# A hybrid attention, pooling and RWKV block on one core: moving the residual gate's matvec to the end of the mixers in half-width pieces, alternating two heads' transposes, and lengthening two planned delays

## The chip, the cores and the metric

The kernel runs on one core of a Trainium2 chip. The metric is the device time of one execution in microseconds. Of the kernel before there are three runs: 1617.52, 1618.55 and 1624.68 us, median 1618.55. The profile is of one more execution, which took 1624.09 us; its trace has a span of 1622.2 us.

## The reference, cut to what matters

One layer on 256 latent tokens with 256 context tokens in front, width 2048, all in float32.

```python
shift_l, scale_l, gate_l = adaln_modulation(c, w_mod, b_mod)   # silu(c) @ w_mod + b_mod, split in three
h = concat(rms_norm(x_ctx) * (1 + scale_c) + shift_c, rms_norm(x_lat) * (1 + scale_l) + shift_l)
parts = split(h @ w_in)                    # q, k, v, gates, pool input, rwkv r, k, v, merge logits ...
y_na = neighbourhood_attention(...)        # 16 heads of 64
y_pool = multiscale_pool(...)
y_rw = rwkv7(...)                          # 16 heads of 64, both directions, seeded by the context
merged = sum(sigmoid(merge_logits[b]) * ((y_b * silu(gate_b)) @ w_branch[b]) for b in range(3))
return rms_norm(x_lat + gate_l * (merged @ w_out), final_g)
```

The change is about three things in it: `gate_l`, a product of one row of 2048 values with a 2048 x 2048 third of `w_mod` that is only needed at the very end; the RWKV part; and the attention.

## The kernel before, in words

The work stands in four stages. **First**, until about 149 us, the modulation's shift and scale are computed piece by piece and the normalised input `hh`, `hl` (a high and a low part of each float32 value) is made for all 16 row blocks. **The mixers**, from 149 to about 1390 us, hold all projections by `w_in` and the three branches. **The merge** multiplies by `w_branch` until about 1528 us, and **the output** by `w_out` until the end.

A projection tile of the mixers (`column_tile`, line 721) is cut in four units. A unit loads 256 KB of weights into a buffer `raw` (line 565), ACT casts it to `whi` (L568), DVE makes the rest `wlo` (L569), and PE does twelve matmuls on it (L738). Most tiles are of latent tokens alone (256 columns); the 48 tiles of the merge gates ("merge tiles", `mth`, `md_`) are such, and nothing in the mixers waits for them, so they are filler. The buffers `raw` are seven, handed out in the order of the program, and all loads go through one queue, SP, that issues in its order and stops at the first one whose buffer isn't free. `whi` and `wlo` have five buffers each.

PE's order is set by a planner written in the kernel (`Order`, line 446). Streams of dependent work (attention and pooling, the RWKV of each of eight pairs of heads) yield pairs: a cost on PE, and a delay until their next step is due. `run` alternates bursts of due steps with projection units. A step with a cost is due again its delay after now; a step without one only adds its delay to its own due time (line 483), so that a stream that has long waited for an event goes on at once, delays or not. `units` (line 1006) keeps three entries loaded ahead. It takes the first entry of the list `todo` whose event has come; an entry without an event can be taken at any time. The order of the other engines and of SP is made by a scheduler from the program.

The gate's product is four entries of that list (`gate_tile`, line 951), one for each 512 columns, all without an event. A unit of it loads 256 KB (`wg`, a buffer of the same seven), and each fourth unit does four matmuls of 32 by 512 (L967) on four column groups of PE, into `mg`, which is in the projections' PSUM buffers. At the end of a tile ACT copies `mg` to `gs` (L972), and 1.2 planned microseconds later PE sums over the groups (`pg`, L946), DVE adds the bias row and the result goes to memory.

The RWKV of a pair makes decays and keys in `features` (up to the copy at L211), then `scores` (`pb`, `pk`, L248 and L250; masked by DVE into `AT` and `EO`), 16 transposes of `BK` (L276) for the two heads of the pair, each head's in a PSUM buffer `pt` that ACT copies out (L277), an inverse on DVE, and a chain of eight steps (`px`, `pu`, `pS`, `py`). The two heads lie in partitions 0 to 63 and 64 to 127. The attention of a pair (`attention`, line 869) does for each half of the queries scores `S` (L887) into two PSUM banks, one of which is shared with the output `po` (L915) of the half before; DVE must have read `po` (L916) before the next `S` can be written.

## Time and profile before

| | us |
|---|---|
| runs before, median (lowest to highest) | 1618.55 (1617.52 to 1624.68) |
| the profiled execution | 1624.09 |
| its span in the trace | 1622.2 |
| PE busy in the span | 1544.7 (95%) |
| DVE busy, ACT busy | 1140.2 (70%), 813.6 (50%) |
| stretch of the gate's matmuls, first to last start | 207.7 to 320.2 |
| the mixers' projections, first to last start | 149.0 to 1389.8 |

The trace gives for each instruction its start and duration and, where an engine was idle before it, what ended the idle time. PE has two rows, the matmuls (PE) and their weight loads (PEld), and a gap is usually seen in both. A float32 matmul that isn't in the rounded form appears as two records. Since a matmul's end is modelled and several overlap, the time that a group holds PE is read from start to next start.

### The profile page before, as it was taken

The page shows a single profiled execution, that of the slowest core. Times are in us where ns is not written, and L with a number is a line of the kernel's source. Part 1 is how long each engine was busy: PE and PEld are TensorE (multiplying, and loading weights), DVE is VectorE, ACT ScalarE, POOL GpSimd, SP SyncE. Part 2 cuts the span into 40 slices and gives each one's busy share as a digit, 9 for nine tenths or more (in the row PEclk, how much of TensorE's full clock was granted, in tenths as well). Part 3 has the DMA queues.
Part 4 walks back from the last instruction along what each step waited for, and adds up shares of the span by engine and source line. Part 5 has one row for each costly group of instructions (what it writes and reads, how often), then busy time and mean ns, then how long its engine had stood idle before and what let it go on. Part 6 is the DMA issues. An engine that isn't in the chain of part 4 may idle for free.

```text
span 1622.2 us, 36488 instructions
## 1 busy us (share of the span) xinstructions
PE 1544.7 (95%) x13848; PEld 1314.9 (81%) x13848; DVE 1140.2 (70%) x2585; ACT 813.6 (50%) x1604; POOL 248.5 (15%) x441
## 2 busy tenths in 40 slices
PE   6999989899999998998999999999899999999998
PEld 4667747388887887877888897787799999999987
DVE  4334875588688788778768878968886554677774
ACT  5224732455364466446446546536644554444553
POOL 2222200140031023023014214003312100000000
PEclk9999999999999999999999999999999999999999
DMA  9997376754433433442442452342366486677892
GB/s 380 331 337 237 111 224 201 231 166 156 144 99 104 146 111 107 134 125 73 137 125 85 153 173 86 105 147 83 106 184 191 163 259 231 221 231 233 271 310 74
DMA packets 201617, 283.26 MB, mean 175 GB/s; under 512 B 67809, under 2 KB 97633, under 8 KB 196833
## 3 DMA queue, kind: packets, MB, share of 16 engines
q1 hardware_dynamic: 201440, 280.93, 53.7%
q8 instruction: 109, 1.79, 0.4%
q14 instruction: 68, 0.55, 0.1%
HBM read 262.24 MB, written 18.35 MB: 173 GB/s over the span
## 4 chain that ended last, share of the span: by engine, by line
PE 78%; DVE 8%; DMA 5%; ACT 4%; issue 3%; SPq 1%; POOL 0%; ACTq 0%; DVEq 0%
PE d L738 43%; PE br L574 3%; PE br L575 3%; PE br L576 3%; PE acc L662 2%; PE psm L614 2%; PE o L574 2%; PE o L575 2%; PE o L576 2%; DMA wg<-in_w_mg 2%; PE acc L665 2%; PE acc L668 2%; DVE wlo L569 2%; DMA bf<-bs 1%; PE pu L387 1%
## 5 line engine op out<-in xcount | busy, mean ns | idle before, releaser
L738 PE MATMUL d<-hh,whi 128*128 128x256 f32 (+1 forms) x1952 | 573.7, 318 | 2.4 <-ACT whi L568 2.2
L568 ACT CAST whi<-raw 128x512 fp32r<-128x512 f32 x584 | 358.5, 620 | 421.8 <-PE d L738 287.5
L738 PE MATMUL d<-hl,whi 128*128 128x256 f32 (+1 forms) x1952 | 553.1, 307 | 0.0
L569 DVE TENSOR_TENSOR wlo<-raw,whi 128x512 fp32r<-128x512 f32 x584 | 404.0, 700 | 175.2 <-ACT whi L568 125.9
L738 PEld LDWEIGHTS d<-hh,whi 128*128 128x128 f32 x1952 | 369.8, 189 | 35.6 <-issue 5.6
L738 PEld LDWEIGHTS d<-hl,whi 128*128 128x128 f32 x1952 | 370.5, 190 | 17.6 <-issue 0.2
L738 PE MATMUL d<-hh,wlo 128*128 128x256 f32 (+1 forms) x1952 | 365.5, 308 | 2.9 <-DVE wlo L569 2.8
L738 PEld LDWEIGHTS d<-hh,wlo 128*128 128x128 f32 x1952 | 287.1, 190 | 22.3 <-DVE wlo L569 3.9
L369 POOL TENSOR_SCALAR sg<-SV,G 64x64 f32<-64x64 f32 x192 | 107.3, 564 | 275.2 <-DVE SV L404 139.5
L574 PE MATMUL br<-bh,whi 128*128 128x256 f32 x384 | 107.9, 281 | 0.0
L575 PE MATMUL br<-bl,whi 128*128 128x256 f32 x384 | 107.9, 281 | 0.0
L576 PE MATMUL br<-bh,wlo 128*128 128x256 f32 x384 | 107.9, 281 | 0.0
L308 DVE TENSOR_TENSOR iM<-iA,iT 128x126 f32<-128x126 f32 (+22 forms) x248 | 65.2, 263 | 12.1 <-DMA iA<-dA 5.6
L576 PEld LDWEIGHTS br<-bh,wlo 128*128 128x128 f32 x384 | 72.4, 188 | 0.0
L574 PEld LDWEIGHTS br<-bh,whi 128*128 128x128 f32 x384 | 72.4, 188 | 0.0
L575 PEld LDWEIGHTS br<-bl,whi 128*128 128x128 f32 x384 | 72.4, 188 | 0.0
L310 DVE TENSOR_TENSOR iT<-iT,iM 128x126 f32<-128x126 f32 (+22 forms) x248 | 64.2, 259 | 6.4
L675 ACT ACTIVATE hh<-xT,md 128x256 fp32r<-128x256 f32 x32 | 17.5, 594 | 88.9 <-DVE md L634 88.9
L1113 DVE TENSOR_TENSOR hl<-rawo,hh 128x512 fp32r<-128x512 f32 x64 | 42.6, 689 | 21.8 <-ACT hh L1112 21.5
L1112 ACT CAST hh<-rawo 128x512 fp32r<-128x512 f32 x64 | 39.3, 621 | 33.2 <-DMA rawo<-in_w_out 15.9
L575 PE MATMUL o<-hl,mh 128*128 128x512 f32 (+1 forms) x144 | 52.6, 366 | 0.0
L574 PE MATMUL o<-hh,mh 128*128 128x512 f32 (+1 forms) x144 | 52.6, 365 | 0.0
(283 smaller groups left out, 2286.6 us busy)
## 6 DMA issues: line engine op xcount, KB each, us to landing
raw<-in_w_in SPq DMA_DIRECT2D x488, 256.0 KB, 3.3
wm<-in_w_ms SPq DMA_DIRECT2D x32, 1024.0 KB, 6.8
raw<-in_w_br SPq DMA_DIRECT2D x96, 256.0 KB, 3.2
wg<-in_w_mg SPq DMA_DIRECT2D x64, 256.0 KB, 4.6
rawo<-in_w_out SPq DMA_DIRECT2D x64, 256.0 KB, 4.3
wst<-in_w_st SPq DMA_DIRECT2D x16, 448.0 KB, 7.5
md__79<-mth SPq DMA_DIRECT2D x48, 128.0 KB, 2.7
mth<-md__79 SPq DMA_DIRECT2D x48, 128.0 KB, 3.1
```

What stands on the lines that cost most here:

```text
L308: nc.vector.tensor_tensor(m, A[:, st:st + 1, st + 1:32].to_broadcast([128, ni, nt]), T[:, 0:ni, st:st + 1].to_broadcast([128, ni, nt]), AL ...
L310: nc.vector.tensor_tensor(T[:, 0:ni, st + 1:32], T[:, 0:ni, st + 1:32], m, ALU.add)
L369: nc.gpsimd.tensor_scalar(sg[hv[par], d], SV[hv[par], par, w, d], G[hv[par], gs[d][0], d:d + 1], None, ALU.mult)
L568: nc.scalar.copy(h, raw)
L569: nc.vector.tensor_tensor(l, raw, h.bitcast(F32), ALU.subtract)
L574: nc.tensor.matmul(acc, a[0], b[0], start=start, stop=False)
L575: nc.tensor.matmul(acc, a[0], b[1], start=False, stop=False)
L576: nc.tensor.matmul(acc, a[1], b[0], start=False, stop=stop)
L614: mm = nc.tensor.matmul(psm[j][32 * g:32 * g + 32, 0:256], cs[:, kt], wm[:, k], start=(kt < 4), stop=(kt >= 12), tile_position=(0, 32 * g))
L738: nc.tensor.matmul(box[0], w[m >= 8][:, 128 * i:128 * i + 128], x, start=(u == 0 and m == 0), stop=(u == 3 and m == 11))
L1112: nc.scalar.copy(hh[kt], raw)
L1113: nc.vector.tensor_tensor(hl[kt], raw, hh[kt].bitcast(F32), ALU.subtract)
```

## The change

The gate's product leaves `todo`. It becomes 64 pieces (`gate_units`), each a load of 256 KB of half the columns (two runs of 1 KB in each partition in place of one of 2 KB); each second piece does four matmuls of 32 by 256. `units` puts one piece behind each projection unit of every tile that it takes once the last attention pair is done (`side7`). A piece counts as one of the three entries loaded ahead. `mg` and `pg` go to the attention's PSUM banks, `gs` and `gb` to its buffers `sl` in place of two `raw` buffers. The 16 transposes of a pair of heads are issued one of each head in turn, both buffers `pt` taken first and copied after all 16. The delay at the end of `features` goes from 2.6 to 3.6, and that behind `po` from 0.3 to 1.0.

```diff
@@ features
         s.BK, s.v = BK, v
-        yield 0.0, 2.6
+        yield 0.0, 3.6
@@ scores
+        pt = [psp.tile([128, 8, 64], F32, tag=ptag, name=f"pt{nm}_{par}") for par in range(2)]
+        for c in range(8):
+            for par in range(2):
+                src = BK[hv[par], c, par:par + 2, :].rearrange("p a t -> p (a t)")
+                nc.tensor.transpose(pt[par][:, c], src, s.ident[hv[par], hv[par]])
         for par in range(2):
-            pt = psp.tile([128, 8, 64], F32, tag=ptag, name=f"pt{nm}_{par}")
-            for c in range(8):
-                src = BK[hv[par], c, par:par + 2, :].rearrange("p a t -> p (a t)")
-                nc.tensor.transpose(pt[:, c], src, s.ident[hv[par], hv[par]])
-            nc.scalar.copy(s.BKT[p, q][:, par], pt.rearrange("p (d c) t -> p d c t", d=2))
+            nc.scalar.copy(s.BKT[p, q][:, par], pt[par].rearrange("p (d c) t -> p d c t", d=2))
@@ attention
                 nc.vector.scalar_tensor_tensor(g[:, c], po, 0.5, g[:, c], ALU.mult, ALU.mult)
-                yield 1.1, 0.3
+                yield 1.1, 1.0
@@ gate
-                wg = wgs[u] = wp.tile([P, 512], F32, tag="raw", bufs=NRAW, name=f"wg{cc}_{u}")
-                nc.sync.dma_start(wg, w_mg[cc, u // 2, :, u % 2])
-                if u % 4 < 3:
+                wg = wp.tile([P, 2, 256], F32, tag="raw", bufs=NRAW, name=f"wg{cc}_{h}_{k}")
+                nc.sync.dma_start(wg, w_mg[cc, k, :, :, 256 * h:256 * h + 256])
+                held.append(wg)
+                if k % 2 == 0:
                     return []
...
-                        nc.tensor.matmul(a[32 * g:32 * g + 32], cs[:, kt], wgs[kt], start=(kt < 4), stop=(kt >= 12),
-                                         tile_position=(0, 32 * g))
+                        nc.tensor.matmul(a[32 * g:32 * g + 32], cs[:, kt], held[i // 2][:, i % 2], start=(kt < 4), stop=(kt >= 12),
+                                         tile_position=(0, 32 * g), skip_group_check=True)
...
-            if p >= 4:
-                todo.append((None, lambda cc=p - 4: gate_tile(cc)))
@@ units
                         cur = todo.pop(i)[1]()
+                        if O.has("side7") and gates:
+                            cur = [x for u in cur for x in [u] + [gates.pop(0) for _ in range(min(GPU, len(gates)))]]
```

How the order changes is shown at three places. The first is the gate's product. On SP before, at the end of its last tile, the loads `wg3_...` follow each other without a projection's load (`raw`) between them:

```order
L957 DMA wg3_8_3227<-in_w_mg 128x512
L957 DMA wg3_9_3229<-in_w_mg 128x512
L957 DMA wg3_10_3244<-in_w_mg 128x512
L957 DMA wg3_11_3246<-in_w_mg 128x512
L957 DMA wg3_12_3248<-in_w_mg 128x512
L957 DMA wg3_13_3250<-in_w_mg 128x512
L957 DMA wg3_14_3268<-in_w_mg 128x512
L957 DMA wg3_15_3270<-in_w_mg 128x512
L565 DMA raw45_3272<-in_w_in 128x512
```

After, late in the mixers, on SP, in the tile of merge gate 35 (`mth34` is the result of the tile before it):

```order
L830 DMA md__79<-mth34_17099 128x256
L958 DMA wg2_1_6_17147<-in_w_mg 128x2x256
L566 DMA raw440_17153<-in_w_in 128x512
L958 DMA wg2_1_7_17171<-in_w_mg 128x2x256
L566 DMA raw441_17173<-in_w_in 128x512
L958 DMA wg3_0_0_17194<-in_w_mg 128x2x256
L566 DMA raw442_17204<-in_w_in 128x512
L958 DMA wg3_0_1_17227<-in_w_mg 128x2x256
L566 DMA raw443_17229<-in_w_in 128x512
L830 DMA md__79<-mth35_17191 128x256
```

And on PE after, where a pair of pieces is used, behind each second projection unit (434 and 435 are units; `mg2` is the third gate tile):

```order
L739 MATMUL d115_17022<-hh6_87,wlo434_17019 128x256
L739 MATMUL d115_17022<-hh7_88,wlo434_17019 128x256
L970 MATMUL mg2_16870<-wg2_1_0_17010,cs_74 32x256 x2
L970 MATMUL mg2_16870<-wg2_1_1_17035,cs_74 32x256 x2
L739 MATMUL d115_17022<-hh8_89,whi435_17039 128x256
L739 MATMUL d115_17022<-hl8_105,whi435_17039 128x256
```

What moved: the 64 gate loads stand no longer in runs early in the mixers but one by one between the loads of the last merge tiles, and their matmuls behind every second projection unit.

The second place is the attention on PE, between the output of the first half of the queries (`po3_0`) and the second half's scores (`S3_0_1`), in pair 3. Before:

```order
L915 MATMUL po3_0_6921<-PT3_0_0_6640,vT3_6580 64x128
L915 MATMUL po3_0_6921<-PT3_0_1_6641,vT3_6580 64x128
L397 MATMUL pS2_1_6931<-SV2_0_5366,BKT2_0_5365 64x64 x4
L887 MATMUL S3_0_1_6942<-kh3_6076,qh3_5861 128x512
L887 MATMUL S3_1_1_6943<-kh3_6076,qh3_5861 128x512
```

After:

```order
L916 MATMUL po3_0_6997<-PT3_0_1_6717,vT3_6656 64x128
L398 MATMUL pS2_1_7007<-SV2_0_5442,BKT2_0_5441 64x64 x4
L108 MATMUL psn3_0_7016<-sq3_0_0_6906,bones_68 128x256
L109 MATMUL psn3_0_7016<-sq3_0_1_6907,bones_68 128x256
L739 MATMUL d91_6847<-hh15_96,whi160_6869 128x256
L739 MATMUL d91_6847<-hl15_112,whi160_6869 128x256
L739 MATMUL d91_6847<-hh12_93,wlo160_6870 128x256
L739 MATMUL d91_6847<-hh13_94,wlo160_6870 128x256
L739 MATMUL d91_6847<-hh14_95,wlo160_6870 128x256
L739 MATMUL d91_6847<-hh15_96,wlo160_6870 128x256
L888 MATMUL S3_0_1_7041<-kh3_6128,qh3_5937 128x512
L888 MATMUL S3_1_1_7042<-kh3_6128,qh3_5937 128x512
```

What moved: six projection matmuls, half a unit, now stand between `po` and `S`. In each of the eight pairs there is at least so much there now; before, five pairs had none.

The third place is the transposes of pair 3 on PE. Before (`x8` is eight equal ones):

```order
L410 MATMUL py2_4_7222<-AT2_1_5895,SV2_1_5897 64x64 x4
L276 MATMUL pt3_0_0_7325<-ident_63,BK3_0_6899 128x64 x8
L276 MATMUL pt3_0_1_7335<-ident_63,BK3_0_6899 128x64 x8
L125 MATMUL psw3_1_7345<-lt0_113,wa3_0_6751 128x256
L125 MATMUL psw3_1_7345<-lt0_113,wa3_1_6752 128x256
```

After:

```order
L411 MATMUL py2_4_7310<-AT2_1_5971,SV2_1_5973 64x64 x4
L276 MATMUL pt3_0_0_7410<-ident_63,BK3_0_6975 128x64
L276 MATMUL pt3_0_1_7411<-ident_63,BK3_0_6975 128x64
L276 MATMUL pt3_0_0_7410<-ident_63,BK3_0_6975 128x64
L276 MATMUL pt3_0_1_7411<-ident_63,BK3_0_6975 128x64
L276 MATMUL pt3_0_0_7410<-ident_63,BK3_0_6975 128x64
L276 MATMUL pt3_0_1_7411<-ident_63,BK3_0_6975 128x64
```

What moved: the two heads' transposes stand in turn, and what follows them (`psw`, which needs the first of the two buffers back) stands behind all 16 as before.

More of the change, by code (lines that the diff above doesn't have):

```diff
@@ L523 @@
 NRAW, NSP, AHEAD = 7, 5, 3
-MOST, LEAST = 2.2, 0.6
+MOST, LEAST, GPU = 2.2, 0.6, 1
 TB = 6
@@ L944, in gate_out @@
             c = slice(512 * cc, 512 * cc + 512)
-            pg = psd.tile([P, 512], F32, tag="d", name=f"pg{cc}")
+            pg = psn.tile([P, 512], F32, tag="o", name=f"pg{cc}")
             nc.tensor.matmul(pg, selg, gs, start=True, stop=True)
@@ L949, in gate_out, with gate_units, load @@
             yield 1.1, 0.0
-        def gate_tile(cc):
-            wgs, box = {}, []
-            def unit_(u):
-                wg = wgs[u] = wp.tile([P, 512], F32, tag="raw", bufs=NRAW, name=f"wg{cc}_{u}")
-                nc.sync.dma_start(wg, w_mg[cc, u // 2, :, u % 2])
-                if u % 4 < 3:
+        def gate_units():
+            held = []
+            def load(cc, h, k):
+                wg = wp.tile([P, 2, 256], F32, tag="raw", bufs=NRAW, name=f"wg{cc}_{h}_{k}")
+                nc.sync.dma_start(wg, w_mg[cc, k, :, :, 256 * h:256 * h + 256])
+                held.append(wg)
+                if k % 2 == 0:
@@ L959, in unit_ @@
                     return []
                 def mult():
-                    if not box:
-                        box.append(psd.tile([P, 512], F32, tag="d", name=f"mg{cc}"))
-                    a = box[0]
-                    for kt in range(u - 3, u + 1):
-                        g = kt % 4
-                        nc.tensor.matmul(a[32 * g:32 * g + 32], cs[:, kt], wgs[kt], start=(kt < 4), stop=(kt >= 12),
-                                         tile_position=(0, 32 * g))
-                    if u == 15:
-                        gs = wp.tile([P, 512], F32, tag="raw", bufs=NRAW, name=f"gs{cc}")
-                        gb = wp.tile([P, 512], F32, tag="raw", bufs=NRAW, name=f"gb{cc}")
-                        nc.scalar.copy(gs, a)
+                    if h == 0 and k == 1:
+                        T["mg"] = psn.tile([P, 512], F32, tag="s", name=f"mg{cc}")
@@ new lines, in mult @@
+                    a = T["mg"][:, 256 * h:256 * h + 256]
+                    for i in range(4):
+                        kt = 2 * k - 2 + i
+                        g = kt % 4
+                        nc.tensor.matmul(a[32 * g:32 * g + 32], cs[:, kt], held[i // 2][:, i % 2], start=(kt < 4), stop=(kt >= 12),
+                                         tile_position=(0, 32 * g), skip_group_check=True)
+                    del held[0:2]
+                    if h == 1 and k == 7:
+                        gs = np_.tile([P, 512], F32, tag="sl", bufs=2, name=f"gs{cc}")
+                        gb = np_.tile([P, 512], F32, tag="sl", bufs=2, name=f"gb{cc}")
+                        nc.scalar.copy(gs, T["mg"])
@@ L973, in mult @@
                         nc.sync.dma_start(gb, rows[0:1, 512 * cc:512 * cc + 512].to_broadcast([P, 512]))
                         O.add(gate_out(cc, gs, gb), 1)
-                    return 1.4
+                    return 0.75
                 return [mult]
-            return [lambda u=u: unit_(u) for u in range(16)]
+            return [lambda cc=cc, h=h, k=k: load(cc, h, k) for cc in range(4) for h in range(2) for k in range(8)]
         todo = []
@@ L1006, in units @@
         def units():
-            ready, cur = [], []
+            ready, cur, gates = [], [], gate_units()
             while True:
@@ L1018, in units @@
                     if not todo:
+                        assert not gates
                         return
```

## The prediction

> **What bounds the kernel now.** I read the page first, then who waited for whom on PE, then the stretches that PE loses.
>
> ```profile
> span 1622.2 us, 36488 instructions
> PE 1544.7 (95%) x13848; PEld 1314.9 (81%) x13848; DVE 1140.2 (70%) x2585; ACT 813.6 (50%) x1604; POOL 248.5 (15%) x441
> ...
> PE 78%; DVE 8%; DMA 5%; ACT 4%; issue 3%; SPq 1%; POOL 0%; ACTq 0%; DVEq 0%
> ```
>
> PE holds 78% of the chain that ended last. Its work stays the same in this change, so the time can only come from places where PE waits or runs slowly. The waits of PE and its weight loads in the mixers (total, times, longest, us):
>
> ```profile
> PE pb L250 <- DVE BK L210: 8.9, 5, 2.4
> ...
> PE S L887 <- DVE gnag L916: 4.6, 4, 1.8
> ...
> PE pg L946 <- ACT gs L972: 3.6, 3, 1.5
> ```
>
> ```profile
> PEld mg L967 <- DMA wg<-in_w_mg: 24.8, 26, 2.6
> ```
>
> The gate's matvec waits for its weights longest of all. Its instructions, and what they waited for (both engine rows added):
>
> ```profile
> L967 PE MATMUL mg<-wg,cs x128: 592/617/1062, 207.7 to 320.2; 128*32 128x512 f32 x128
> ...
>   DMA wg<-in_w_mg: 31.5, 34
> ...
> DMA to landing us min/median/max: 2.5/4.6/6.6
> ```
>
> How it waits, in PE's timeline (start, duration, idle before):
>
> ```profile
> 288.66 1.06 PE L967 MATMUL mg<-wg,cs 128*32 128x512 f32 x8
> 289.66 0.45 PE L387 MATMUL pu<-xs,AT 64*64 64x64 f32 x8
> ...
> 307.71 1.72 PE L967 MATMUL mg<-wg,cs 128*32 128x512 f32 x4 [1.32 <-DMA wg<-in_w_mg]
> ...
> 311.08 1.61 PE L967 MATMUL mg<-wg,cs 128*32 128x512 f32 x6
> 313.32 1.05 PE L967 MATMUL mg<-wg,cs 128*32 128x512 f32 x2 [0.63 <-DMA wg<-in_w_mg]
> 315.07 3.06 PE L967 MATMUL mg<-wg,cs 128*32 128x512 f32 x8 [0.71 <-DMA wg<-in_w_mg]
> ```
>
> Eight records, four matmuls on four loads, need 1.0 us (288.66 to 289.66) when the weights are there. With seven buffers and four held by a multiplication, the fourth load of the next one can only start when it is over; so each comes some 4 us behind the last (311.08, 315.07) for 1.0 us of work.
>
> **The change part by part.** The sum is made against the profiled execution, 1624.1 us with 1622.2 of span; it lies 5.5 us above the median of the runs, 1618.55, and I take the difference from the median.
>
> *Gate, early: what goes.* The wait is 24.8 us by the weight loads' row, 31.5 if the two rows never show the same gap; they mostly do, so I take 25. Merge tiles come there instead. Two waits of others behind the gate's loads in SP's queue go too:
>
> ```profile
> 230.61 0.39 PE L738 MATMUL d<-hh,whi 128*128 128x256 f32 x1 [1.82 <-ACT whi L568]
> ...
> 299.81 0.38 PE L125 MATMUL psw<-lt,wa 128*128 128x256 f32 x1 [0.92 <-ACT wa L80]
> ```
>
> 2.7 us, and with smaller ones I take 3 (2 to 5). PE's own work doesn't change: the matmuls are twice as many and half as wide, and the first stage has the same form:
>
> ```profile
> 70.47 1.07 PE L614 MATMUL psm<-wm,cs 128*32 128x256 f32 x16
> ```
>
> 16 records in 1.07 us are 0.5 us for a piece pair of eight, 32 times 16 us as now. The three waits of `pg` for ACT, 3.6 us, stay, since ACT copies as before.
>
> *Gate, late: what comes.* Now each load of a piece lies in SP's queue and in the seven buffers between two projection loads, and is held until its matmul. Behind it queue the next projection loads, the merge results' stores and, once, the transfers of the last inverse. Counting seven on from the first two pieces of a pair of units, the loads for the next-but-one pair start when that multiplication is over. From there PE has one more pair of units and a multiplication to do. The rows for this loop, at the end of the mixers where only merge tiles run (first all engines, then the instructions on `raw`):
>
> ```profile
> 1280.00:1295.00 15.00, 15.00 (x130) 15.00 (x129) 10.63 (x18) 10.70 (x19) 0.00 (x0) 1.00 0.53 176
> ```
>
> ```profile
> L568 ACT CAST whi<-raw x32: 611/620/622, 1230.0 to 1289.2; 128x512 fp32r<-128x512 f32 x32
> ...
> DMA to landing us min/median/max: 3.0/3.1/4.2
> ```
>
> 15 us for 130 matmuls are 1.4 us for a unit of twelve, so a tile of four units and two multiplications is 6.6 us of PE. The loop is the landing L, 0.6 for the cast, 0.2 (an estimate from the gaps between rows) for the signals, two units and a multiplication, 3.3: L + 4.1. It costs L − 2.5 a tile: 0.6 us at 3.1, the median here, nothing at 2.5, 2.1 at the 4.6 of `wg`, 4.1 at its longest, 6.6. Of 16 tiles, the first half also has the last pair's chain between its units, which covers 0.6 us. So 8 × 0.6 = 5 us, ends 0 and 16 × 2.1 = 34. I take the low side, since the loads come evenly. What two runs of 1 KB cost in place of one of 2 KB has no row for a load of this size; the upper end holds it. The delay of `gs` by ACT's casts, the banks of `mg` and `pg` and the buffers of `gs` and `gb` I cost at nothing: the attention, whose they are, is over when the first piece is loaded, and `pg` has half a unit of projection in front of it as cover; without that, four waits of 0.6 us, the cast's time, would be added. They are 2 MB in 6.6 us and a store of 0.13, 340 GB/s, and the DMA engines can do that:
>
> ```profile
> 0.00:50.00 50.00, 35.58 (x271) 26.11 (x271) 19.66 (x46) 22.34 (x33) 11.65 (x21) 1.00 0.94 370
> ```
>
> 370 GB/s at a share of 0.94. The Trainium skill ("DMA: Bandwidth & Descriptors", Where 436 GB/s comes from) gives about 358 GB/s of HBM for a core; by that the late stage has 5% to spare, and by this row, which exceeds it, 8% and more.
>
> *Delay behind `po`.* At pair 2 the scores follow the output with only a short group between and wait for DVE to read `po` out of the shared bank; the clock then drops:
>
> ```profile
> 457.01 0.50 PE L887 MATMUL S<-kh,qh 64*128 64x512 f32 x1
> 459.31 0.46 PE L887 MATMUL S<-kh,qh 64*128 64x512 f32 x1 [1.80 <-DVE gnag L916]
> ```
>
> ```profile
> 226.00:240.00 14.00, 10.65 (x56) 6.04 (x55) 10.36 (x36) 2.19 (x4) 0.00 (x0) 0.76 0.71 225
> ...
> 459.00:465.00 6.00, 5.69 (x40) 4.79 (x40) 4.35 (x11) 3.44 (x6) 1.30 (x2) 0.72 0.48 154
> ...
> 770.00:778.00 8.00, 6.88 (x54) 6.31 (x55) 6.67 (x13) 3.41 (x6) 0.00 (x0) 0.57 0.39 134
> 1158.00:1164.00 6.00, 4.73 (x46) 4.16 (x47) 4.89 (x10) 2.06 (x4) 0.00 (x0) 0.72 0.27 90
> ```
>
> Half a unit more now stands there, 0.7 us, in each of the four cases of 4.6 us: 4 × 0.7 = 2.8, and the stretch at granted clock 0.72, 0.28 × 6 = 1.7, ends if the wait falls from 1.8 to 1.1. I take 4 (0 to 6). The Trainium skill ("TensorE: Matmul & The Clock Gate", What's actually happening) halves the clock after an idle window of about 3.4 us; by it neither wait would drop it, and there would be 1.7 us less to win. The trace drops it after 1.8, and I go by the trace.
>
> *Delay of 3.6.* It is meant for the wait of `pb` for `BK`, 8.9 us. But `features` has waited there for the chain of the pair before, and all its later steps have no cost, so their delays add to a due time that is long past (line 483). The new order bears this out: for pairs 1 and 3 the same number of projection matmuls stands between that chain's end and `pb`, for 4 and 5 some 26 to 30 fewer, for 2, 6 and 7 between 6 and 30 more. The wait stays in most pairs:
>
> ```profile
> 767.57 0.60 PE L905 MATMUL pt<-ident,sl 128*128 128x128 f32 x4
> 770.57 0.43 PE L250 MATMUL pb<-EO,BK 64*64 64x128 f32 x2 [2.40 <-DVE BK L210]
> ```
>
> I take −2 for pair 7 (the slow stretch at 1158 with it), ends −6 and +4.
>
> *Transposes in turn.* Both heads' now, one head after the other:
>
> ```profile
> 218.51 0.95 PE L276 MATMUL pt<-ident,BK 64*128 64x64 f32 x16
> 219.40 1.06 PE L967 MATMUL mg<-wg,cs 128*32 128x512 f32 x6
> ```
>
> 16 in 0.89 us, in 16 blocks 14 us. The Trainium skill ("TensorEngine Tiling (Array Packing)", Key Properties) says that tiles of rows load weights and multiply in parallel; by it half, 7 us, would go. No row here has this form in turn, so the ends are 0 and 7. The last of DVE's reads of the scores is now waited for by the second transpose and not the ninth, and ACT's first copy starts later, which takes part back. I take 3.
>
> Sum: −25 −3 +5 −4 −2 −3 = −32. From the median, 1618.5 − 32 = **1586 us**.
>
> **The rivals.** *A, the wait only moves.* If loads land in 4.6 us, as `wg` did, the loop costs 2.1 us in all 16 tiles, 34 and not 5: 1586 + 29 = 1615. For it: the projection loads get half of the seven buffers. Against: `wg` landed so late in bursts of loads, and the window of merge tiles has 3.1. The Trainium skill ("DMA: Bandwidth & Descriptors", Latency and other measured facts) has HBM access rise from 0.2 to 2 us at high load, which would bring 3.1 to about 4.9 here (an estimate). 7%.
>
> *B, slower.* The same loop at the longest landing, 6.6: 4.1 × 16 = 66 us, 61 more, 1647. It decides when a tile loses more than (32 + 5 + 8) / 16 = 2.8 us, a landing of 5.3. Against: only the longest `wg` was so. 4%.
>
> *C, more is won.* Shorter waits everywhere also end the other slow-clock stretches (770 alone is 0.43 × 8 = 3.4 us), the transposes go in parallel (4 more), and the late loop costs nothing (5): −12, 1574. 20%.
>
> *D, it does less than it says.* The gaps of the gate cover work of DVE and ACT that is late next: the merge tiles in their place need a cast and a subtraction each 1.4 us, and the first pairs then wait as the later ones do. Against: in the window at 1280 the same tiles leave DVE a third of its time. Half of the 28 early is lost: 1600. 10%.
>
> **How the numbers follow.** The forecast has 59%. The range, 1564 to 1606: down, C with 31.5 for 25 and `pb` at its end (6.5 + 4 below 1574); up, D with 6 of the transposes and `po` gone. A and B lie above it, 11%. About 0.5%, 8 us, is what a measurement can tell from no change here (the three runs span 7). Faster by more, below 1610.5: forecast, C and D, 89%; same: most of A, 6%; slower: B and a little of A, 5%.
>
> **What would show it.** After, between 207 and 325 us no `mg`, and PE at the pace of the neighbouring windows; `mg` matmuls between about 1120 and 1280 us; the wait `mg <- wg` under 5 us and the projections' wait for `whi` in that stretch 3 to 10; `S <- gnag` under 2; `pb <- BK` still 6 to 10; 16 transposes in 0.45 to 0.9 us. The prediction is wrong if PE loses over 20 us late or if the early stretch keeps gaps of another kind.

## The result, and the profile after

The changed kernel took 1633.49 us (median of five runs, 1631.74 to 1638.14) against 1619.16 for the kernel before in the same session: a ratio of 1.0083, 95% interval 1.0056 to 1.011. It is slower by about 13 us; the forecast was 32 us faster. Its profiled execution has a span of 1630.7 us, 8.5 more than before. The page of the changed kernel, first lines and the chain by engine:

```profile
span 1630.7 us, 36672 instructions
PE 1539.9 (94%) x13976; PEld 1318.9 (81%) x13976; DVE 1136.5 (70%) x2585; ACT 809.2 (50%) x1600; POOL 244.5 (15%) x441
...
PE 27%; DMA 6%; DVE 5%; ACT 2%; issue 1%; SPq 0%; ACTq 0%; DVEq 0%
...
PE d L739 9%; DMA raw<-in_w_in 4%; PE br L577 3%; PE br L575 3%; PE br L576 3%; PE o L577 2%; PE o L575 2%; PE o L576 2%; DVE wlo L570 2%; DMA bf<-bs 1%; ACT whi L569 1%; DVE iM L309 0%; PE mg L970 0%; DVE iT L311 0%; PE pu L388 0%
```

On this page the chain is followed back only to 962 us, so its shares add up to 41% of the span and can't be set beside those of the kernel before, whose chain reaches back to the start. In the stretch that both have, 960 to 1400 us, the loads of `raw`, the projections' weights, make up 16.4% of the chain after, and before it has one of them:

```profile
1217.18 3.63 DMA raw<-in_w_in
```

The gate itself went where it should (its matmuls, and what they waited for, in the changed kernel):

```profile
L970 PE MATMUL mg<-wg,cs x256: 379/403/637, 1188.4 to 1347.0; 128*32 128x256 f32 x128
...
  DMA wg<-in_w_mg: 1.5, 2
...
DMA to landing us min/median/max: 2.8/4.1/6.0
```

31.5 us of waits have become 1.5. What took their place is in the waits of PE over the whole execution (total, times, longest, us). Before:

```profile
PE d L738 <- ACT whi L568: 2.2, 2, 1.8
...
PE pt L276 <- DVE EO L268: 1.3, 2, 1.0
```

And after:

```profile
PE d L739 <- ACT whi L569: 11.6, 13, 4.2
PE pt L276 <- DVE EO L268: 9.6, 7, 2.6
PE pb L250 <- DVE BK L210: 9.0, 4, 3.2
...
PE S L888 <- DVE gnag L917: 2.1, 2, 1.4
```

The projections wait for their casts, 11.6 us for 2.2, the transposes for DVE, 9.6 for 1.3. `S` waits less, 2.1 us where under 2 was forecast, and `pb` as long as before. ACT, one step back, late in the mixers (1140 to 1400 us), shows why the projections wait. Before:

```profile
ACT whi L568 <- PE d L738: 76.2, 91, 2.4
...
ACT whi L568 <- DMA raw<-in_w_in: 7.0, 7, 1.9
```

And after:

```profile
ACT whi L569 <- DMA raw<-in_w_in: 86.6, 52, 5.3
ACT whi L569 <- PE d L739: 26.0, 26, 3.3
```

Before, ACT waited for PE to free `whi`: loads were ahead. After, ACT waits for the loads and PE waits for ACT. From issue to cast a load took 8.6 us in the median before (1170 to 1320 us, worked out from the issues and the casts in their order), of which it lay 5 us ready. After it is 4.1 us, all of it the landing, as the row for `raw` from 1160 to 1370 us of the changed kernel has it (its median is 3.4 us before):

```profile
DMA to landing us min/median/max: 2.9/4.1/7.8
```

One place is worse than the rest. The last pair's inverse sends eight small transfers through SP; SP and then PE of the changed kernel:

```profile
1196.75 3.78 SPq L321 DMA_DIRECT2D AT<-dT  x8
1200.63 0.40 SPq L830 DMA_DIRECT2D md__79<-mth  x1
1201.12 0.38 SPq L566 DMA_DIRECT2D raw<-in_w_in  x1
```

```profile
1200.03 0.39 PE L739 MATMUL d<-hh,whi 128*128 128x256 f32 x1 [2.17 <-ACT whi L569]
...
1205.90 0.58 PE L739 MATMUL d<-hh,whi 128*128 128x256 f32 x1 [4.18 <-ACT whi L569]
```

```profile
1205.00:1219.00 14.00, 13.10 (x171) 11.49 (x172) 4.80 (x8) 5.28 (x10) 0.00 (x0) 0.51 0.64 206
```

The wait of 2.17 us is for a load that SP issued at 1195.21, ahead of these transfers. The next projection load is issued only at 1201.12, behind the transfers and a store. None is ready, so PE stands for 4.18 us, and then runs for 14 us at a granted clock of 0.51.

**Where the time went.** The time from the first `pb` of the last block of scores (pair 7, second half) to the merge's first `br`, worked out from starts of matmuls. A projection matmul of 256 columns holds PE for 0.118 us when the next is ready; "lost" is the time of the projection matmuls beyond that. The last column is the time at a halved granted clock between 240 and 1400 us.

```
kernel            last pb   first br   projection matmuls   us     lost   half clock in the mixers
before            1158.4    1390.0     1674                 209.5  12.0   20.5
after             1139.8    1397.6     1458                 206.7  34.7   47.8
e1_gate_only      1120.2    1386.3     1530                 216.0  35.5   20.5
e7_own_buffers    1126.5    1377.0     1530                 201.5  21.0   27.3
e11_own_16        1118.3    1362.7     1530                 197.8  17.3   10.2
```

With the gate alone moved (e1), this block starts 38 us earlier and 144 more projection matmuls, 17 us, are already done; so the early part gains 55 us, 47 of them the time that `mg` held PE before. Of these the late part takes back 25.6 us for the gate's matmuls and 23.5 us of new losses among the projections (35.5 against 12.0). The changed kernel loses as much late, and comes to this block 20 us later than e1, with only 72 more matmuls (8.5 us) done: 11 us lost early, by the other parts of the change.

The last tiles with pieces hold nothing but merge work. From one group of `mg` to the next but one, such a tile takes 8.2 us in the changed kernel and 8.9 in e1 (means of the last seven), where the forecast's loop had 6.6 and 0.6 of waiting.

**The granted clock in all runs.** Every run has its granted clock on record. It is 0.983 in the mean of the changed kernel's five runs and 0.9915 in that of the 112 runs of the kernel before that stand beside the experiments. Time multiplied by granted clock is what would be left if each half-clock stretch lost half of its length: 1607.1 us after and 1607.3 before, a difference of −0.2 ± 1.5. So, by this reckoning, the change wins as much as it loses apart from the clock, and its 13 us stand in the clock. This is an upper bound for the clock, since PE also waits in such stretches; among the runs of the kernel before, 0.01 less clock goes with 13.6 us more time, where 16 would be the whole of it.

### The profile page after: what moved, and what is told of

The parts are those of the page before. It is cut to its first block, busy times and chain, and to the rows that moved or that the text cites. A ratio compares the mean times of both kernels' runs of the same rounds, so it can differ in the third digit from the quotient of the medians.

```text
span 1630.7 us, 36672 instructions
## 1 busy us (share of the span) xinstructions
PE 1539.9 (94%) x13976; PEld 1318.9 (81%) x13976; DVE 1136.5 (70%) x2585; ACT 809.2 (50%) x1600; POOL 244.5 (15%) x441
## 5 line engine op out<-in xcount | busy, mean ns | idle before, releaser
L739 PE MATMUL d<-hh,whi 128*128 128x256 f32 (+1 forms) x1952 | 585.0, 323 | 11.9 <-ACT whi L569 11.6
L405 DVE SCALAR_TENSOR_TENSOR SV<-pS,G,sg 64x64 f32<-64x64 f32 x192 | 46.0, 279 | 12.6 <-PE pS L398 10.7
```

Of the source, the lines that this page charges most:

```text
L405: nc.vector.scalar_tensor_tensor(o, pS[hv[par], d], g, sg[hv[par], d], ALU.mult, ALU.add)
L739: nc.tensor.matmul(box[0], w[m >= 8][:, 128 * i:128 * i + 128], x, start=(u == 0 and m == 0), stop=(u == 3 and m == 11))
```

## The experiments

All ratios are to the kernel before, run beside each kernel; 0.001 is 1.6 us.

### The parts apart

Four kernels. *e1_gate_only* is the kernel before with only the gate's pieces:

```diff
-            if p >= 4:
-                todo.append((None, lambda cc=p - 4: gate_tile(cc)))
...
+                        if O.has("side7") and gates:
+                            cur = [x for u in cur for x in [u] + [gates.pop(0) for _ in range(min(GPU, len(gates)))]]
```

> The kernel before with the gate's 64 pieces alone; transposes and both delays as before. Theory A (the pieces win some 25 us early and lose as much late behind the loads of SP's queue; the transposes in turn cost the rest): 1614 to 1624 us against 1619, no change to speak of. Theory B (the gate's move is all of the loss, and transposes and delays win a few us as forecast): 1636 to 1642. The forecast's own reckoning for this part, minus 23: 1596.

*e2_transposes_only* is the kernel before with the changed lines of `scores` alone:

```diff
+        for c in range(8):
+            for par in range(2):
...
+                nc.tensor.transpose(pt[par][:, c], src, s.ident[hv[par], hv[par]])
```

> The kernel before with the two heads' transposes in turn alone. Theory A: slower by 8 to 15 us, 1627 to 1634, with the waits of the transposes for DVE's last reads (EO, L262 and L268) three times as long and more stretches at half clock. Theory B: 3 to 7 us faster, 1612 to 1616.

*e3_delays_only* is the kernel before with the two delays:

```diff
-        yield 0.0, 2.6
+        yield 0.0, 3.6
...
-                yield 1.1, 0.3
+                yield 1.1, 1.0
```

> The kernel before with the delays 3.6 and 1.0 alone. Theory A and B alike: 1 to 5 us faster, 1614 to 1618, the wait of S for po (4.6 us) halved and the wait of pb for BK as it was. A change of over 8 us either way would mean that the new order of the steps itself, not what was costed, sets the time.

*e4_no_transposes* is the changed kernel with the transposes of the kernel before:

```diff
-        pt = [psp.tile([128, 8, 64], F32, tag=ptag, name=f"pt{nm}_{par}") for par in range(2)]
...
+            pt = psp.tile([128, 8, 64], F32, tag=ptag, name=f"pt{nm}_{par}")
```

> The changed kernel with the transposes of one head after the other, as before; gate pieces and delays stay. Theory A: 10 to 15 us faster than the changed kernel, 1618 to 1624, as long as the kernel before. Theory B: 3 to 7 us slower than the changed kernel, 1636 to 1641.

Measured: e1 1.0012 (0.9993 to 1.0032), e2 1.0053 (1.0027 to 1.0078), e3 1.0059 (1.0043 to 1.0075), e4 1.0075 (1.0054 to 1.0096). The gate moves no time at all, and both other parts lose, where each was forecast to win a little. e3 moves by more than the 8 us that its expectation named, and e4 lies in neither of its ranges. The parts don't add up either: 1.0012, 1.0053 and 1.0059 would make 1.012 and not 1.0083. In time multiplied by clock, against the kernel before, e1 has −2.0 us (± 2.0), e2 +2.6, e3 +1.7 and e4 −1.2 (each ± 1.2); the clock has the rest, 3.0, 8.0, 8.3 and 12.7 us.

e3 has one long wait that the kernel before does not have. PE around 300 us, and SP ahead of it:

```profile
308.71 1.73 PE L125 MATMUL psw<-lt,wa 128*128 128x256 f32 x4 [6.25 <-ACT wa L80]
```

```profile
289.82 7.46 SPq L957 DMA_DIRECT2D wg<-in_w_mg  x10
...
300.00 0.60 SPq L78 DMA_DIRECT2D wa<-in_wa  x1
```

With other delays the pair's `wa` was needed while its load stood behind the gate's, which are still early in e3. The wait of 6.25 us, and a stretch of 6.8 us at half clock that begins in it, at most 3.4 us more, are as much as e3's 9.5 us. That nothing else counts is not shown: all of its mixers have 30.7 us at half clock against 20.5. In e1 and in the changed kernel, where the gate has moved, PE has no such wait for `wa`.

### What holds up the late loads

Four kernels on e1. *e5_quarter_loads* loads a quarter of each piece's columns and multiplies them four times over, so that it leaves out the other three quarters of the gate's weights:

```diff
-                nc.sync.dma_start(wg, w_mg[cc, k, :, :, 256 * h:256 * h + 256])
+                nc.sync.dma_start(wg[:, :, 0:64], w_mg[cc, k, :, :, 256 * h:256 * h + 64])
```

> The gate pieces alone, each loading only the first 64 of its 256 columns and multiplying them four times over, so that the output's gate is not the reference's, while PE's work, the buffers and the order stay. Theory R (the late loss is the order: pieces take half of the seven buffers and stand in SP's queue): no change from the gate pieces alone, 1618 to 1623 us. Theory L (the loss is the load on the DMA engines, which makes every projection load land late, 4.4 for 3.1 us): landings of raw back under 3.5 us, the wait of the projections for whi (14.3 us) under 6, and 1606 to 1612.

*e6_start_half7* begins the pieces at another of the planner's events:

```diff
-                        if O.has("side7") and gates:
+                        if O.has("half7") and gates:
```

> The gate pieces alone, begun when the chain of the last pair is half done and not when the last attention is over, so that none stand in SP's queue around the transfers of the last inverse (AT). Both theories of the steady loop leave this part out: if those transfers hold the projection loads up because the pieces have used up the lead, the two waits of 2.9 and 2.8 us and the half-clock stretches near them go, 1610 to 1616 us; if not, 1619 to 1623.

*e7_own_buffers* takes the pieces out of the seven shared buffers, into four of the attention's:

```diff
-                wg = wp.tile([P, 2, 256], F32, tag="raw", bufs=NRAW, name=f"wg{cc}_{h}_{k}")
+                wg = np_.tile([P, 2, 256], F32, tag=("PT", "kt")[k // 2 % 2], bufs=2, name=f"wg{cc}_{h}_{k}")
```

> The gate pieces alone, loaded into four buffers of the attention, so that the seven of raw are the projections' again and SP issues projection loads three units earlier. Theory R: the wait for whi under 5 us and 1604 to 1612. Theory L: the same bytes in the same time, the wait stays near 14 us, 1617 to 1623.

Measured: e5 0.996 (0.9945 to 0.9974), e6 1.0131 (1.0108 to 1.0154), e7 0.9926 (0.9903 to 0.9949). e7 takes 14 us from e1 and is faster than both kernels. ACT's late waits (1140 to 1400 us), in e1:

```profile
ACT whi L568 <- DMA raw<-in_w_in: 98.2, 55, 5.2
ACT whi L568 <- PE d L738: 14.5, 17, 1.7
```

In e7 they have the order of the kernel before again:

```profile
ACT whi L568 <- PE d L738: 86.3, 80, 4.7
ACT whi L568 <- DMA raw<-in_w_in: 14.8, 6, 6.6
```

The windows 1280 to 1320 us, before, e1 and e7, show that it was not the transfers' rate (PE, PEld, DVE, ACT, POOL busy; clock; DMA share; GB/s):

```profile
1280.00:1320.00 40.00, 39.43 (x330) 38.85 (x328) 23.12 (x33) 24.66 (x41) 0.00 (x0) 1.00 0.71 236
```

```profile
1280.00:1320.00 40.00, 35.04 (x293) 28.63 (x294) 13.83 (x20) 13.17 (x24) 0.00 (x0) 1.00 0.81 260
```

```profile
1280.00:1320.00 40.00, 39.19 (x332) 32.38 (x331) 14.91 (x22) 15.01 (x28) 0.00 (x0) 1.00 0.90 297
```

e1 leaves PE idle for 5 of 40 us at 260 GB/s, e7 keeps it busy at 297. The pieces land in 4.2 us in e7 and in 4.3 in e1. So it is not the landing that costs, but where a projection load stands: behind pieces that hold four of its seven buffers until they are multiplied. e5, whose pieces land in 2.9 us, gets 8 us of the 14, which puts it between the ranges of the two theories: with the same buffers and the same order, a shorter landing of the pieces helps too, presumably since they give their buffers back sooner.

e6 was expected to be no slower than e1 by either theory, and lost 19 us. The pieces start no earlier there but later (first `mg` at 1226.5 us, e1 1166.7), and run to the end of the mixers, 1367.3. The merge's first inputs `bf` are then loaded at 1378.2 us (e1 1340.8), and PE waits for their casts, 1360 to 1420 us:

```profile
PE br L574 <- ACT bh L1046: 12.5, 3, 5.3
PE br L575 <- DVE bl L1047: 3.5, 2, 1.7
```

So pieces at the very end put off the merge; whether `bf` is late by its place in SP's queue or by the memory that it needs was not tried.

*e8_gate_po_delay* is e1 with the delay behind `po` at 1.0:

```diff
-                yield 1.1, 0.3
+                yield 1.1, 1.0
```

> The gate pieces and the delay of 1.0 behind po, without that of 3.6 and without the transposes in turn. Gate pieces with both delays took 1632, gate pieces alone 1621. If the delay behind po makes the 11 us (by shifting the later steps, the wait of pb for BK above all), 1629 to 1634 here; if the delay of 3.6 makes them, 1616 to 1622.

Measured: 1.0039 (1.0025 to 1.0053), 4 us over e1, between the two ranges. `S` waits for `gnag` 2.1 us on PE, 2.5 less than before. But e1 has no such wait on PE at all: on the gate alone there is nothing left for this delay to shorten.

### Buffers, lookahead or switches

*e9_after_own* is the changed kernel with e7's line for `wg`.

```diff
-                wg = wp.tile([P, 2, 256], F32, tag="raw", bufs=NRAW, name=f"wg{cc}_{h}_{k}")
+                wg = np_.tile([P, 2, 256], F32, tag=("PT", "kt")[k // 2 % 2], bufs=2, name=f"wg{cc}_{h}_{k}")
```

> The whole change (gate in pieces, transposes in turn, both delays), with the gate's pieces in four attention buffers as in e7_own_buffers. Theory of the held-up loads (a piece's load stands in the one queue and takes one of the seven shared buffers ahead of a projection's): the gain of e7 over e1 (0.9926 against 1.0012) comes off here too, 1614 to 1624 us, and ACT's waits of whi for raw late in the mixers fall from 87 us to under 25; what is left over e7 is the transposes and the delays, some 8 to 14 us. Rival, that the longer delays leave too few projection units for the late stretch and it waits whatever the buffers are: 1628 to 1634.

*e10_own_64* is e7 with each piece multiplied by itself:

```diff
-                if k % 2 == 0:
-                    return []
...
-                    for i in range(4):
-                        kt = 2 * k - 2 + i
+                    for i in range(2):
+                        kt = 2 * k + i
```

> e7_own_buffers, but each piece is multiplied as soon as it is there: 64 groups of 2 matmuls between projection units in place of 32 groups of 4, the same matmuls and loads. Theory of the switch (each change from the projections' wide matmuls to the gate's narrow ones and back costs PE 0.25 to 0.3 us beyond the matmuls): 32 more switches, 8 to 10 us over e7, 1613 to 1619. Rival, that the short gaps at the switches are only the pipeline's ends and would lie elsewhere: as e7, 1604 to 1610.

*e11_own_16* is e7 with four pieces multiplied at once:

```diff
-                wg = np_.tile([P, 2, 256], F32, tag=("PT", "kt")[k // 2 % 2], bufs=2, name=f"wg{cc}_{h}_{k}")
+                tag = ("PT", "PT", "kt", "kt", "vT", "sl", "sl", "raw")[k]
...
-                if k % 2 == 0:
+                if k % 4 < 3:
...
-                    for i in range(4):
-                        kt = 2 * k - 2 + i
+                    for i in range(8):
+                        kt = 2 * k - 6 + i
```

> e7_own_buffers, but four pieces are multiplied at once: 16 groups of 8 matmuls, with seven attention buffers and one of the shared ones for the pieces. Theory of the switch: 16 switches fewer, 4 to 5 us under e7, 1600 to 1604. Rival: as e7, 1604 to 1610, or slower where the matmuls wait for the last of four loads.

*e12_ahead6* is e1 with more entries loaded ahead:

```diff
-                while len(ready) < AHEAD:
+                while len(ready) < (2 * AHEAD if gates and O.has("side7") else AHEAD):
```

> e1_gate_only (pieces in the seven shared buffers), but six entries are kept loaded ahead instead of three while there are pieces. Every other entry is a piece, so three ahead are only one or two projection units. Theory of the lookahead: three units ahead again, as good as e7, 1605 to 1611. Theory of the shared buffers: six entries and the two pieces held don't fit the seven buffers, loads wait for buffers, 1617 to 1624 as e1.

Measured: e9 0.9987 (0.9971 to 1.0003), e10 1.0014 (0.9994 to 1.0033), e11 0.9883 (0.9854 to 0.9912), e12 0.9998 (0.9982 to 1.0014).

e9 falls as far below the changed kernel as e7 below e1, 0.0096 and 0.0086: the shared buffers cost as much in the whole change. e12 is e1's time: the short lookahead isn't the cause. From issue to cast a load takes 4.4 us there as in e1, and 10.8 in e7.

The switches have a price. 32 more cost 0.0088, 14 us (9 to 19 by the two intervals, more than the 8 to 10 that were expected), and 16 fewer win 0.0043, 7 us (1 to 13; e11's buffers differ too, seven of the attention's and one of the shared). With the clock taken out these are 17.9 and 4.9 us, each ± 2.7: 0.56 us for a switch more and 0.31 for one fewer. PE's timeline shows what a switch is; e10, e7 and e11, one group and the matmuls behind it each:

```profile
1242.48 0.62 PE L966 MATMUL mg<-wg,cs 128*32 128x256 f32 x4
1243.04 0.39 PE L738 MATMUL d<-hh,whi 128*128 128x256 f32 x1
1243.26 0.28 PE L738 MATMUL d<-hl,whi 128*128 128x256 f32 x1
```

```profile
1248.47 0.64 PE L969 MATMUL mg<-wg,cs 128*32 128x256 f32 x8
1249.04 0.39 PE L738 MATMUL d<-hh,whi 128*128 128x256 f32 x1
1249.27 0.28 PE L738 MATMUL d<-hl,whi 128*128 128x256 f32 x1
```

```profile
1255.23 1.07 PE L970 MATMUL mg<-wg,cs 128*32 128x256 f32 x16
1256.23 0.39 PE L738 MATMUL d<-hh,whi 128*128 128x256 f32 x1
```

Four records hold PE for 0.56 us, from start to next start, eight for 0.57, sixteen for 1.00: a short group costs as much as one twice as long. And the first projection matmul behind a group holds PE for 0.22 us instead of 0.118. By these rows two groups of four cost 0.65 us more than one of eight, and two of eight 0.24 more than one of sixteen, close to the prices above. e11 is the fastest of these kernels, 1603.94 us in the median.

### The transposes

In e2 the order of PE's 13,848 matmuls is that of the kernel before, name for name, but for the order among the transposes. There are 16 blocks of them, one for each pair of heads and half (3_0 is pair 3, first half; the expectations call the blocks pairs). Set beside each other, e2 falls back by 0.8 to 2.3 us at four of the 16, 3_0, 3_1, 5_1 and 7_0. At 7_1 the first head waits too, but what follows is no later. At the first of them, PE before:

```profile
606.70 0.71 PE L276 MATMUL pt<-ident,BK 64*128 64x64 f32 x8
608.08 0.71 PE L276 MATMUL pt<-ident,BK 64*128 64x64 f32 x8 [0.68 <-ACT BKT L277]
```

DVE before, which reads `pk` for the last time here:

```profile
608.27 0.42 DVE L262 TENSOR_TENSOR EO<-pk,mk 64x256 f32<-64x256 f32 x1
```

And PE in e2:

```profile
606.99 0.27 PE L276 MATMUL pt<-ident,BK 64*128 64x64 f32 x1
609.04 0.71 PE L276 MATMUL pt<-ident,BK 64*128 64x64 f32 x15 [1.78 <-DVE EO L262]
```

The fifteen behind the wait take the 0.71 us that eight took before: tiles of rows in turn do run in parallel, 32 ns from start to start against 56. But they can't start. `pb`, `pk` and `pt` share two PSUM banks (the compiled program lists them), and the change takes one bank for each head. The Trainium skill ("TensorEngine Tiling (Array Packing)", Gotcha 1: PSUM Pressure) says that different row tiles write to different banks and can't access one at the same time; no run here puts two heads in turn into one bank. The second bank is the one that `pk` leaves, and it is free only when DVE has read `pk` to the end. Before, only the second head waited for it, and at three blocks (3_0, 3_1, 7_0) not even that, since both heads went through the first bank. In turn, the first head waits too.

*e13_two_banks* claims both banks ahead, head by head:

```diff
+        pt = [psp.tile([128, 8, 64], F32, tag=ptag, name=f"pt{nm}_{par}") for par in range(2)]
         for par in range(2):
-            pt = psp.tile([128, 8, 64], F32, tag=ptag, name=f"pt{nm}_{par}")
```

> The kernel before, with one thing changed: the transposes' two tiles are both claimed ahead of the first transpose, as in the change; the transposes stay head by head, each head's copy behind its eight. The compiled program gives every pair's two heads different PSUM banks then, where before three of the 16 pairs (3_0, 3_1, 7_0) put both heads through one bank. Theory of the bank (the second bank is the one that pk leaves, and it comes free only behind the last EO on DVE): the second head waits 0.5 to 1 us longer at three pairs, 1622 to 1625 us against 1621, and the rest of the loss of e2_transposes_only (1632) comes from issuing in turn, which makes the first head's transposes wait for that bank too. Rival, that the claim alone makes the loss: 1629 to 1634. Rival, that neither matters and the in-turn issue is slow by itself: 1619 to 1622.

*e14_turn_eleven* and *e16_turn_five* split the blocks:

```diff
+        if (p, q) not in ((3, 0), (3, 1), (5, 1), (7, 0), (7, 1)):
...
+                    nc.tensor.transpose(pt[par][:, c], src, s.ident[hv[par], hv[par]])
+        else:
```

> The kernel before with the transposes in turn in eleven of the 16 pairs only; the five pairs 3_0, 3_1, 5_1, 7_0 and 7_1, at which e2_transposes_only (same order of PE otherwise) fell back by 1.0 to 2.0 us each in the trace because the first head's transposes waited for the bank of pk, stay head by head. Theory of the wait: no loss is left and the faster issue (0.3 us a pair, eleven pairs) shows or is hidden, 1616 to 1621 us. Rival, that issuing in turn is slow by itself (copies later, row tiles): eleven sixteenths of e2's loss, 1625 to 1629.

> The other half: in turn in the five pairs 3_0, 3_1, 5_1, 7_0 and 7_1 only. Theory of the wait: the whole loss of e2_transposes_only, 1627 to 1633 us. Rival: five sixteenths of it, 1622 to 1624.

Measured: e13 0.9998 (0.9983 to 1.0014), e14 0.997 (0.9952 to 0.9988), e16 1.0058 (1.0036 to 1.008). The claim by itself costs nothing, less than I had expected. In turn at eleven blocks it wins 5 us; at the other five it makes the whole loss of e2. So the loss comes from issuing in turn where the bank comes late, and not from issuing in turn as such. The wait itself is the smaller part of it: with the clock taken out e16 loses 3.0 us (± 1.3) and e14 wins 0.7 (± 1.2), and the other 6.0 and 3.6 us are clock. In e14's trace the eleven blocks are shorter by 0.8 us in all, so the gain that was forecast is hardly there. And 3.1 us of e2's lag arise at 700 us, away from any transpose: `mp` waits 2.56 us for ACT's copy `mP`, before 0.92. What brings that on stays open; e14, which wins, waits 2.09 us there.

### The delays

*e15_gate_scores_delay* is e1 with the delay ahead of the scores at 3.6; *e17_own16_short* is e11, and *e18_short_delay* the kernel before, with it at 1.6:

```diff
-        yield 0.0, 2.6
+        yield 0.0, 1.6
```

> e1_gate_only with the delay ahead of the scores at 3.6 instead of 2.6, the other delay as before. Gate and both delays stood at 1.0075, gate and the delay behind po at 1.0039, gate alone at 1.0012. Theory of sums: the rest is this delay's, 1625 to 1629 us. Theory of the planner (a delay planned longer than the work behind it takes draws a projection unit ahead of the step, and the pair's step then comes late by up to a unit of 2.3 us): the same sign, and PE's waits for BK at pb stay at 6 to 10 us. Rival, that this delay does what it is for: pb's waits under 4 us and 1614 to 1620.

> e11_own_16 (the fastest so far, 0.9883) with the delay ahead of the scores at 1.6 instead of 2.6. Theory of the planner: a shorter delay draws fewer units ahead of the scores, so the steps come earlier but wait longer for BK; 1600 to 1606 us, with pb's waits above 10 us. Rival, that any shorter delay is a gain (the opposite of what the longer one did): 1594 to 1600.

> The kernel before with the delay ahead of the scores at 1.6 instead of 2.6 and nothing else. If the gain of e17 over e11 (0.9843 against 0.9883, intervals that touch) is this delay's own, it shows here too: 1612 to 1618 us. Rival, that a delay only reshuffles which waits fall where and has no sign of its own: 1618 to 1628.

Measured: e15 1.0 (0.998 to 1.0019), e17 0.9843 (0.9809 to 0.9877), e18 1.0085 (1.0056 to 1.0113). On the gate alone the longer delay costs nothing, with the other delay it costs (e4 1.0075, e8 1.0039). Before, both a longer and a shorter one stand in slower kernels; on e11 the shorter one is, if anything, faster, though the two intervals overlap. e17 lies below both of its ranges and e18 above both. So the theory that the delays lose by a sign of their own falls. That they decide which waits become long, and that this depends on everything else in the order, fits these runs but was not tried by itself. e17 is the fastest kernel of the study, 1593.64 us.

## Why the prediction was wrong, point by point

**The early gate: right.** −25 and −3 were forecast. Of the 47.0 us that `mg` held PE before, 16 were work by the prediction's own count and 31 waits; e1's early part gains the 47 and 8 more. No stall of another kind took their place (rival D): the pairs' scores come 30 us earlier from the second pair on, and 38 at the last.

**The late loop: the step that failed.** The prediction took the landing of the late loads at 3.1 us, the row of a stretch without the gate's loads, and said that "the first half also has the last pair's chain between its units", so that only 8 of 16 tiles pay: +5. The runs show 23.5 us of new losses among the projections, and 25.6 us for the gate's matmuls where 16 had been counted, together 33 in place of 5. Three things were wrong in this term. The landing in the stretch is 4.1 us for both kinds of load, which by the prediction's own L − 2.5 is 1.6 a tile, a tile of 8.2 us, and 26 us in 16 tiles. The tiles of merge work alone take just that, 8.2 us (8.9 in e1). So the loop was seen rightly and fed a landing from a stretch without pieces, and rival A's mechanism, given 7%, was the likelier. The chain's transfers do not cover anything; they are in the same queue, and the eight of `AT` stand ahead of the longest wait, 4.18. And the narrow groups were costed at their pace in a long run, "16 records in 1.07 us"; what a short group and the switch behind it cost was not in the sum. The loss has two parts: the shared buffers (e7 and e9 win 14 and 16 us back, 12 and 8 with the clock taken out) and the short groups (with own buffers, in e9, five of the last seven tiles still take 7.2 us where the sum had 6.6: some 10 us in 16 tiles).

**The clock: put at nothing.** The sum priced the half clock only at a wait that it meant to end, 1.7 us. What new waits would cost in clock had no term. With the late loop put right alone, 33 for 5, the sum would still be −4; measured are +13, and by the reckoning of the runs above all of that stands in the clock. With the clock taken out the gate has −2.0 us, the two delays on top of it +0.8 and the transposes on top of those +1.0, where −23, −6 and −3 were forecast.

**The delay behind `po`: the wait had gone with the gate.** −4 was taken, with ends 0 and 6. On the kernel before the delays do shorten the wait of `S`, 2.1 us in e3 instead of 4.6. But the gate's move alone ends it on PE (e1), and with this delay on top it is 2.1 us again and the kernel 4 us slower (e8). The parts were priced one by one on the kernel before, and not on each other.

**The delay of 3.6: the wait stays, as said.** `pb <- BK` (DVE) is 9.0 us after, 8.9 before, but not by standing still: it is 4.3 in e1, 3.8 in e15 and 7.3 in e8. Its price, −2 with ends −6 and +4, holds alone on the gate (−2, e15 against e1); with the other delay the two cost 10 us (e4 against e1), which the ends of the two terms together, −12 to +4, did not hold.

**The transposes: a loss that the ends left out.** "The last of DVE's reads of the scores is now waited for by the second transpose and not the ninth" was written down, and then bounded at 0. Five blocks cost 9 us, two thirds of it by the clock, and decide the term; at the other eleven −5 was measured, inside the 0 to −7 of the faster issue, but by luck, since most of it is clock. On top of gate and delays the part costs only 1 us (1.0083 against 1.0075), within the intervals of the two.

In ratios the changed kernel is then 1.0012 for the gate (55 us won early, 49 lost late), +0.0063 for both delays on it, +0.0008 for the transposes on those. The two delays cost 10 us together and 4 and −2 singly. With the clock taken out they cost 0.8 us together and win 2.3 and 2.1 singly, all within ± 3, and the clock takes 9.7, 7.6 and 0.6: e4 runs 44.4 us of the mixers at half clock, e8 34.1, e15 and e1 20.5. Which of the new waits brings each half-clock stretch stays open.

## What to carry to other kernels

Filler that is moved into a late stretch should bring its own buffers: in a shared ring behind one queue it takes away the loads' head start before it takes any bandwidth, and issue to use, set against the landing, shows that in one line. Interleave in groups long enough to pay for the switch. Read each run's granted clock beside its time: here it holds nearly all of the difference between the two kernels. And before two independent chains are issued in turn, look at which buffer the second takes and who reads it last, since in turn the first chain waits for that as well.

## What the runs showed of the hardware

**The clock goes by a window's busy share.** In the 20 profiled executions (before, after and the experiments), the half-clock stretches between 150 and 1560 us are 3.41 us long or a multiple of it, on one grid in each execution. With PE's busy share in the window ahead worked out from the matmuls, and that window at full clock, the clock was halved behind 49 of 49 windows under 0.4, 44 of 53 from 0.4 to 0.5, 20 of 84 from 0.5 to 0.6, 12 of 179 from 0.6 to 0.7, and 7 of some 7,700 above. Behind a window that is at half clock itself the share says less: of 161 such windows over 0.7, 29 were followed by another at half clock. The Trainium skill ("TensorE: Matmul & The Clock Gate", What's actually happening) has a free-running window of 3413 ns, which these agree with; it speaks of an idle window, and here one that is half idle is enough. A wait of some 2 us may thus cost 1.7 us more, or nothing, by where it falls. Two examples of the changed kernel, PE ahead of the scores of blocks 1_1 and 4_1, and the window around the latter:

```profile
344.78 0.51 PE L250 MATMUL pb<-EO,BK 64*64 64x128 f32 x2 [1.98 <-DVE BK L210]
```

```profile
738.77 0.69 PE L250 MATMUL pb<-EO,BK 64*64 64x128 f32 x2 [3.25 <-DVE BK L210]
```

```profile
735.00:745.00 10.00, 6.19 (x61) 4.93 (x60) 7.81 (x18) 2.90 (x7) 0.00 (x0) 0.66 0.27 90
```

The mixers of the changed kernel have 47.8 us at half clock against 20.5 in e1 and before: at most 13.7 us of work lost, where its span is 12.1 longer than e1's. No experiment changes the clock alone.

**A short group of narrow matmuls has a floor.** Four records of 32 by 256 hold PE as long as eight, 0.56 and 0.57 us, sixteen 1.00, and the full-width matmul behind them twice as long as its like.
